# Seven half-size products summed in two pairs of PSUM banks

## The chip, the cores and the metric

The kernel runs on one core of one Trainium2 chip. The metric is the device time of one execution in microseconds. A core has five engines, each of which works off its own instructions in order: TensorE (PE, with its weight loads shown as PEld), VectorE (DVE), ScalarE (ACT), GpSimd (POOL) and SyncE (SP), whose queue issues most of the DMAs. Matmuls write only to PSUM, which here is used as eight banks of 128 x 512 float32; DVE and ACT read results from there.

## The reference

One inference step of a two-layer decoder trunk on 1056 token columns: 1024 prompt tokens and 8 sequences of 4 new tokens.

```python
def _hgrn_layer(x, g_norm, w_in, lb, o_gain, w_out, S0):
    xn = _rmsnorm(x, g_norm)
    u = (xn @ w_in).astype(jnp.float32)
    q, f, iv, gate = jnp.split(u, 4, axis=-1)
    q = jax.nn.silu(q).reshape(Bsz, T, H_B, DK_B)
    log_g = jnp.logaddexp(jnp.log(lbh), jnp.log1p(-lbh) + jax.nn.log_sigmoid(f...))
    k = -jnp.expm1(log_g)
    v = iv.reshape(Bsz, T, H_B, DV_B)
    o, S_T = _hgrn2_chunked(q, k, v, log_g, S0)
    o = o * lax.rsqrt(jnp.mean(o * o, axis=-1, keepdims=True) + EPS) * o_gain
    y = (o.reshape(Bsz, T, INNER_B) * jax.nn.silu(gate)).astype(x.dtype)
    return x + y @ w_out, S_T
```

Layer 1 is an RG-LRU layer (input projection, causal convolution, gates, scan, output projection). Layer 2 is the HGRN2 layer above: model width 1024, 8 heads, 128 keys and 128 values per head. Then comes a final RMSNorm. The change touches layer 2's input projection `xn @ w_in` and PSUM's use around it.

## The kernel before, in words

Each float32 operand is split into a high and a low part of a type that TensorE multiplies at full rate, so one product of two 128 x 128 x n blocks is three matmuls (`mm3`: high x high, high x low, low x high).

Layer 2 needs, for each head h and each of four kinds (0 query, 1 forget gate, 2 value V, 3 output gate), a product of a 1024 x 128 weight block with 1024 x 1056 activations. For most heads two kinds at a time, `a` and `b`, are done in one call of `seven`: together they form a 2 x 2 block product (two kinds, two halves of the inner dimension, two halves of 528 columns, `HT`), and it is done with seven half-size products in place of eight (Winograd's form). There are 13 calls: one for head 1 (kinds 3 and 2), two for each of heads 2 to 7. The columns of a product are again done in two parts of 264 (`QT`), x = 0 and 1; each takes twelve matmuls into one PSUM bank.

Within a call, products are numbered 1 to 7 and run in the order of a string: `GV0` (once, head 1), `FQ` (query and forget gate) and `GV` (gate and V). A "b" in the string is a place for a burst: the attention work of this head and the one before, in four bursts a head. Bursts 1 and 2 stand in the gate/V call and work on levels of this head's decay (`levels01`, `levels24`) and on the states of the head before (`states`, `advance`); bursts 3 and 4 stand in the query/forget call of the next head. In burst 2 the state matmuls come after the first half of the product that follows the "b". Masked copies (`keep`, `keep_s`, L1142 and L1145) take the level products out of PSUM.

PSUM before: the seven products rotate through three banks (`mm`), the bursts through the other five (`hg`). Each half of a product is read as soon as it is done: product 1 by an ACT copy (L1570), the others by a DVE addition `plus` (L1598) of the bank and an earlier partial sum in SBUF, written back to SBUF. The partial sums lie in six places of 264 columns in one large tile `KR` (shown as k). Product 5 has two additions per half, the others one, so a call has 14 additions and 2 copies. The last additions for V write V itself (`VT`). `ending` and `settle` then apply the activation on ACT from the finished sum in SBUF: Silu for query and gate (L1612), a Tanh and two scalings for the forget gate (L1606 to L1608). For the query and forget kinds that waits until one or two bursts have passed, since the bursts still read the rows to be overwritten. `own_gate` (L1150, DVE) multiplies the finished query by the decay.

Weights come by four DMAs per call into five raw places (`rawq`); DVE forms the sums that the seven products need (`combine`), ACT casts each to its high part (L1522), POOL subtracts to get the low part (L358). `NW` = 4 of these pairs are ahead; the next split is put in line after each product.

The order on each engine is written out by a planner, class `Flow`. Every operation is added with its engine, an assumed duration, and the keys that it reads and writes. PE's operations run in program order; the others are ordered by list scheduling with due times found backwards from the end, and additions and activations of the seven products have the first priority (0). The plan is made anew when the operations change. An operation's real waits come from the tiles that it touches. Layer 1 uses the four `mm` banks as a ring of four; after the seven products the output projection uses a ring of three (`banks8[:NMM]`).

Of the kernel before, what the change touches and what calls it, by code (L numbers as in the profile page):

```python
# [27 lines left out]
K1 = 5  # L28
NMM = 3
HC = 2  # L30
NM7 = 3
GV0, FQ, GV = "126b743b5", "12b675b43", "126b754b3"
CUT = 2
SPOTS, SPOTS0, SPOTS1 = (-1, -1, 0, 2), (2, 5, -1, -1), (1, 5, 9, 13, 17, 20)
K2 = 8 - K1
# [5 lines left out]
SEQ = 1024  # L41
# [8 lines left out]
H = 8  # L50
# [187 lines left out]
def tile_trunk(ctx: ExitStack, tc: tile.TileContext, xT, prm, hc, w0, wg, wo0, w1, wo1, s_in,  # L238
# [25 lines left out]
    def chunk(c):  # L264
        return slice(c * CH, (c + 1) * CH)

    def mm3(out, w, xh, xl, first, last):
        wh, wl = w
        T.matmul(out, wh, xh, start=first, stop=False)  # L269
        T.matmul(out, wh, xl, start=False, stop=False)  # L270
        T.matmul(out, wl, xh, start=False, stop=last)  # L271

    def run(*gens):
        for g in gens:
            for _ in g:
                pass
# [53 lines left out]
    with ExitStack() as l0:  # L330
# [9 lines left out]
        def banks(tag, n):  # L340
            return cycle([(psum.tile([128, 512], F32, tag=tag, bufs=n, name=tag), (tag, i)) for i in range(n)])
# [4 lines left out]
        def act(n, emit, r, w, prio=5, more=0.0):  # L346
            fl.add("ACT", 0.08 + 0.00086 * n + more, emit, r, w, prio)
# [47 lines left out]
        sgr = cycle(slots)  # L395
        YH = [fixed(f"yh{j}", [128, TOK], F32R) for j in range(3)]
        YL = [fixed(f"yl{j}", [128, TOK], F32R) for j in range(3)]
        mm, hg = banks("mm", 4), banks("hg", 4)

        def xpart(j, i, c):  # L400

# [603 lines left out]
    with ExitStack() as l1:  # L1005
# [488 lines left out]

        def seven(h, a, b, order, at=()):

            nonlocal rawq, places
            bursts, passed, postponed, rest = iter(at), 0, [], None

            def ending(i, *args):  # L1500
# [38 lines left out]
            combine("12", "12", "11", ALU.subtract)  # L1539
            for p in steps[2:NW]:  # L1540
                split(p)
            late, mid, low = places
            places = low, mid, late
            for c in order:
                if not c.isdigit():
                    rest = next(bursts)()
                    passed += 1
                    flush()
                    continue
                p = int(c)  # L1550
                if p == steps[-1]:
                    rawq = freed
                hi, lo, wk = parts[p]
                for x in range(2):
                    ps, pk = next(mm)
                    ops = [operand(p, j, x) for j in range(4)]

                    def emit(ps=ps, ops=ops, hi=hi, lo=lo):
# [8 lines left out]
                    z = ps[:, :QT], pk  # L1567
                    first, second = x * QT, HT + x * QT
                    if p == 1:
                        act(QT, lambda o=late[x][0], z=z[0]: S.copy(o, z), (pk,), (late[x][1],), 0)  # L1570
                    elif p == 2:
                        plus(mid[x], z, late[x])
                        ending(a, first, *mid[x])
                    elif p == 6:
                        plus(late[x], z, late[x])
                    elif p == 7:
                        plus(low[x], z, late[x])
                    elif p == 3:
                        plus(late[x], z, late[x])
                    else:  # L1580
                        t, o = second if p == 5 else first, mid[x] if next(q for q in steps if q in (4, 5)) == p else low[x]
                        if b == 2:
                            plus((VT[:, t:t + QT], ("VT", t // QT)), z, low[x])
                            if t + QT == TOK:
                                thrice("vs", VT[:, SEQ:], (("VT", 3),))
                        else:
                            plus(o, z, low[x])
                            ending(b, t, *o)
                        if p == 5:
                            plus(late[x], z, late[x])  # L1590
                    if p == [q for q in steps if q in (3, 5)][1]:
                        ending(a, second, *late[x])
                n = steps.index(p) + NW
                if n < 7:
                    split(steps[n])

        def plus(o, z, u):
            dve(QT, lambda: V.tensor_tensor(o[0], z[0], u[0], op=ALU.add), (z[1], u[1]), (o[1],), 0)  # L1598

        def settle(h, i, a, c, ck):  # L1600

            q = slice(a, a + QT)
            if i == 1:
                b, bk = brow(h, 1)
                b, bk, g = b[:, q], bk[a // QT::4], ("G", a // QT)
                act(QT, lambda: S.activation(b, c, AF.Tanh, scale=0.5), (ck,), bk, 0)  # L1606
                act(QT, lambda: S.activation(Gs[:, q], b, AF.Identity, bias=lbc[:, h:h + 1], scale=lc[:, h:h + 1]), bk, (g,), 0, 0.2)
                act(QT, lambda: S.activation(b, b, AF.Identity, bias=lc[:, h:h + 1], scale=lcn[:, h:h + 1]), bk, bk, 0, 0.2)  # L1608
            else:
                o, k = (SG[h], ykeys(h % 2, a, QT)) if i else arow(h, 0)  # L1610
                k = k if i else k[a // QT::4]
                act(QT, lambda: S.activation(o[:, q], c, AF.Silu), (ck,), k, 0)  # L1612


        dma(si.rearrange("p b v -> p (b v)"), s_in[0], (), two("si"), 4, 512)
# [34 lines left out]
        places = []  # L1650
        for i in range(6):
            key = ("s", i)
            inherit(key, [("k", j) for j in range(5) if j * CH < (i + 1) * QT and (j + 1) * CH > i * QT])
            places.append((KR[:, i * QT:i * QT + QT], key))
        places = places[:2], places[2:4], places[4:]
        rawq = [next(raws) for _ in range(NRAW)]
        for i in range(5 - NRAW):
            key = ("W", i)
# [42 lines left out]
        own = []  # L1701
        for i, o in enumerate(ks):
            key = ("k", i, 1)
            inherit(key, [("s", j) for j in range(6) if j * QT < (i + 1) * CH and (j + 1) * QT > i * CH])
# [239 lines left out]
```

## Time and profile before

| | us |
|---|---|
| median of three runs | 1028.95 |
| lowest, highest | 1027.11, 1031.18 |
| span of the profiled execution | 1027.8 |
| TensorE busy in it | 1015.8 |
| VectorE busy | 808.0 |
| ScalarE busy | 573.2 |
| GpSimd busy | 504.2 |

For the profiled execution the span is given, from its first to its last instruction; no other time of it is listed. The calls of `seven` lie at about 559 to 906 us. In the rows of the profile, "line engine op out<-in shapes xcount | busy us, mean ns of one | idle time of the engine before them <- what ended it" is a group; a timeline row is "start us, duration us, engine line op"; a row of stretches is "from:to length, then busy us (x instructions) of PE, PEld, DVE, ACT, POOL, then TensorE's granted clock, DMA share and GB/s". An engine line with q (SPq) is its queue. The names before and after "<-" are tiles; mm and hg are PSUM.

### The profile page before, as it was taken

To read this page: it belongs to the slowest core of one execution; us is meant where nothing else is said; L and a number is where in the kernel's file an instruction comes from. 1 tells how busy PE (TensorE), PEld (TensorE's weight loads), DVE (VectorE), ACT (ScalarE), POOL (GpSimd) and SP (SyncE) were. 2 spreads that over 40 slices of the span, in tenths; PEclk is the share of its full clock that TensorE was granted. 3 is DMA by queue.
4 is the path that set the end of the run, shared out by engine and by line. 5 is a ranking of instruction groups with operands and counts; after the bars stand their busy time and mean duration, and the time that the engine had idled before them with its cause. 6 is when DMAs were issued, how large, how long until landed. Compare 5 with 4: busy or idle time off the path is not lost.

```text
span 1027.8 us, 26439 instructions
## 1 busy us (share of the span) xinstructions
PE 1015.8 (99%) x10100; PEld 995.2 (97%) x10100; DVE 808.0 (79%) x1640; ACT 573.2 (56%) x1313; POOL 504.2 (49%) x580
## 2 busy tenths in 40 slices
PE   9999999999999999999999999999999999999997
PEld 9999999999999999999999999999999999999986
DVE  7998987689788689344598989888989898986436
ACT  7688566877765766344454463626363545552324
POOL 1324454454446345635425555555565656633544
PEclk9999999999999999999999999999999999999999
DMA  9211112213762487553564245443535353777204
GB/s 303 73 51 37 54 57 66 79 53 104 222 198 70 131 267 241 157 173 130 159 192 136 72 131 149 130 148 112 167 107 172 94 166 114 217 230 229 88 1 169
DMA packets 109582, 139.95 MB, mean 136 GB/s; under 512 B 24208, under 2 KB 86800, under 8 KB 109456
## 3 DMA queue, kind: packets, MB, share of 16 engines
q1 hardware_dynamic: 107440, 135.84, 42.7%
q10 hardware_dynamic: 2016, 2.43, 0.7%
q8 instruction: 79, 1.29, 0.5%
q14 instruction: 47, 0.39, 0.1%
HBM read 90.02 MB, written 41.61 MB: 128 GB/s over the span
## 4 chain that ended last, share of the span: by engine, by line
PE 87%; DVE 4%; DMA 4%; ACT 2%; issue 1%; POOL 1%; SPq 1%; POOLq 0%; ACTq 0%; DVEq 0%
PE mm L269 25%; PE mm L271 24%; PE mm L270 24%; PE hg L1138 2%; DMA R<-td 1%; PE hg L269 1%; PE hg L270 1%; PE hg L271 1%; PE hg L1340 1%; PE hg L1285 1%; PE hg L1342 1%; DMA wraw<-in_w_dram 1%; DMA k<-x1a 1%; SPq L344 1%; DMA R<-in_xT_dram 1%
## 5 line engine op out<-in xcount | busy, mean ns | idle before, releaser
L269 PE MATMUL mm<-xh,whi 128*128 128x352 f32 (+1 forms) x1127 | 349.9, 311 | 0.0
L271 PE MATMUL mm<-xh,wlo 128*128 128x352 f32 (+1 forms) x1127 | 347.8, 309 | 0.0
L270 PE MATMUL mm<-xl,whi 128*128 128x352 f32 (+1 forms) x1127 | 347.7, 309 | 0.0
L358 POOL TENSOR_TENSOR wlo<-wraw,whi 128x256 fp32r<-128x256 f32 (+3 forms) x188 | 201.9, 1090 | 194.6 <-ACT whi L418 93.7
L269 PEld LDWEIGHTS mm<-xh,whi 128*128 128x128 f32 x1127 | 211.7, 188 | 1.2 <-DVE k L1598 0.2
L270 PEld LDWEIGHTS mm<-xl,whi 128*128 128x128 f32 x1127 | 212.3, 188 | 0.4
L271 PEld LDWEIGHTS mm<-xh,wlo 128*128 128x128 f32 x1127 | 212.0, 188 | 0.0
L269 PE MATMUL mm<-t,whi 128*128 128x264 f32 (+1 forms) x330 | 96.6, 293 | 0.0
L544 DVE SCALAR_TENSOR_TENSOR k<-xb,prm_sb,k 128x352 f32<-128x352 f32 (+2 forms) x144 | 87.3, 633 | 10.4 <-ACT k L541 9.6
L271 PE MATMUL mm<-t,wlo 128*128 128x264 f32 (+1 forms) x330 | 94.5, 286 | 0.0
L270 PE MATMUL mm<-t,whi 128*128 128x264 f32 (+1 forms) x330 | 94.3, 286 | 0.0
L1598 DVE TENSOR_TENSOR k<-mm,k 128x264 f32<-128x264 f32 x154 | 64.1, 424 | 11.9 <-PE mm L271 10.5
L358 POOL TENSOR_TENSOR wlo<-R,whi 128x256 fp32r<-128x256 f32 x70 | 57.1, 838 | 27.8 <-ACT whi L1522 24.6
L1522 ACT CAST whi<-wraw 128x512 fp32r<-128x512 f32 x56 | 34.6, 617 | 58.6 <-DVE wraw L1532 31.0
L637 POOL TENSOR_TENSOR k<-X 128x352 f32<-128x352 f32 x36 | 43.8, 1222 | 45.4 <-DVE R L638 33.6
L269 PEld LDWEIGHTS mm<-t,whi 128*128 128x128 f32 x330 | 62.0, 188 | 2.1 <-ACT kt L1355 0.9
L271 PEld LDWEIGHTS mm<-t,wlo 128*128 128x128 f32 x330 | 62.2, 188 | 0.0
L270 PEld LDWEIGHTS mm<-t,whi 128*128 128x128 f32 x330 | 62.1, 188 | 0.0
L418 ACT CAST whi<-wraw 128x512 fp32r<-128x512 f32 (+2 forms) x79 | 43.8, 571 | 27.3 <-PE mm L270 20.0
L269 PE MATMUL mm<-yh,whi 128*128 128x352 f32 x153 | 49.9, 326 | 1.0 <-DVE k L689 1.0
L270 PE MATMUL mm<-yl,whi 128*128 128x352 f32 x153 | 49.4, 323 | 0.0
L271 PE MATMUL mm<-yh,wlo 128*128 128x352 f32 x153 | 49.4, 323 | 0.0
(484 smaller groups left out, 2503.1 us busy)
## 6 DMA issues: line engine op xcount, KB each, us to landing
wraw<-in_w_dram SPq DMA_DIRECT2D x89, 256.0 KB, 3.1
wraw<-in_wo_dram SPq DMA_DIRECT2D x34, 192.0 KB, 2.6
R<-in_w_dram SPq DMA_DIRECT2D x17, 256.0 KB, 3.5
si<-in_s_in_dram SPq DMA_DIRECT2D x8, 512.0 KB, 5.5
vt<-sg SPq DMA_DIRECT2D x8, 512.0 KB, 3.7
kt<-kt SPq DMA_DIRECT2D x8, 512.0 KB, 3.3
sg<-vt SPq DMA_DIRECT2D x32, 128.0 KB, 2.9
kt<-kt SPq DMA_DIRECT2D x32, 128.0 KB, 4.5
```

The source lines that it names most:

```text
L269: T.matmul(out, wh, xh, start=first, stop=False)
L270: T.matmul(out, wh, xl, start=False, stop=False)
L271: T.matmul(out, wl, xh, start=False, stop=last)
L344: fl.add("SP" if q is Q else "ACT", us, lambda: q.dma_start(dst, src), r, w, prio, kb * (1.0 if r else 0.75))
L358: emit = lambda: e.tensor_tensor(b, x, a.bitcast(F32), op=ALU.subtract)
L418: act(m, lambda hi=hi, raw=raw, m=m: S.copy(hi[:, :m], raw[:, :m]), rk, (hk,), prio)
L544: dve(u, lambda src=src, dst=dst, sh=sh, k=k: V.scalar_tensor_tensor(dst, sh(src, k), pc("cw", 12 * k + m), dst, op0=ALU.mult, op1=ALU.add ...
L637: pool(CH, lambda x=x, a=a, b=b: G.tensor_tensor(x, a.bitcast(F32), b.bitcast(F32), op=ALU.add), (ak, bk), (xk,), 3)
L1138: T.matmul(ps[32 * j:32 * j + 32, n * w:n * w + w], B[:, o:o + 32], q(slice(o, o + 32)), start=True, stop=True, tile_position=(0, 32 * j))
L1285: T.matmul(ps[w, n * 128:(n + 1) * 128], kt[:, 4 * i + n, a], vt[:, 4 * i + n], start=True, stop=True, tile_position=(0, 32 * a))
L1522: act(512, lambda: S.copy(hi, raw), (rk,), (hk,), 2)
L1598: dve(QT, lambda: V.tensor_tensor(o[0], z[0], u[0], op=ALU.add), (z[1], u[1]), (o[1],), 0)
```

## The change

The seven products of a call are summed in two pairs of PSUM banks. Products 1, 6, 7 and 4 go to one pair ("chain"), 2, 5 and 3 to the other ("side"). Only 1, 2 and 5 start afresh; the others add onto what lies in the pair. Bank 0 of a pair holds x = 0, bank 1 x = 1, and one instruction reads both (528 columns). ACT copies the pair out after 1, after 6 and after the first of 5 and 7; DVE adds the pair to an SBUF sum after 2, after 3 and after the second of 5 and 7: three additions a call. After 4 the sum is complete in PSUM and its activation reads it from there. Chain and side change places from call to call. The partial sums have three places of 528 columns. All of `settle` works on 528 columns, and V is written by an ACT copy.

Around it: the seven products have four banks (`NM7`) and the bursts four; `burst2` takes its third bank after the level products; the orders of the products are others; in each call the two kinds have changed places (forget gate and V are now `a`, which is finished by products 2 and 3; query and gate are `b`, finished by 5 or 7, and 4). The four `mm` banks are allocated as two tiles of two banks.

```diff
-NM7 = 3
-GV0, FQ, GV = "126b743b5", "12b675b43", "126b754b3"
+NM7 = 4
+GV0, FQ, GV = "126b754b3", "12b657b34", "126b573b4"
...
-        mm, hg = banks("mm", 4), banks("hg", 4)
+        PP = [psum.tile([128, 2, 512], F32, tag="mm", bufs=2, name="mm") for _ in range(2)]
+        mm, hg = cycle([(PP[i // 2][:, i % 2], ("mm", i)) for i in range(4)]), banks("hg", 4)
...
         def burst2(h):
             s = next(hg)
+            run(together([levels24(h, *s)] if h < H else []))
             t = next(hg) if h < H else s
-            run(together([levels24(h, *s)] if h < H else []))
...
-            late, mid, low = places
-            places = low, mid, late
+            one, two_, five = places
+            banks2 = [(PP[i], [("mm", 2 * i), ("mm", 2 * i + 1)]) for i in range(2)]
+            chain_, side = banks2[turns % 2], banks2[1 - turns % 2]
+            turns += 1
...
+            def copied(o, z):
+                act(HT, lambda: S.copy(halved(o[0]), z[0][:, :, :QT]), z[1], (o[1],), 0)
+            def plus(o, z):
+                dve(HT, lambda: V.tensor_tensor(halved(o[0]), z[0][:, :, :QT], halved(o[0]), op=ALU.add), (*z[1], o[1]), (o[1],), 0)
...
+                z = chain_ if p in (1, 6, 7, 4) else side
                 for x in range(2):
-                    ps, pk = next(mm)
+                    ps, pk = z[0][:, x], z[1][x]
...
-                            mm3(ps[:, :QT], (hi[:, w], lo[:, w]), uh, ul, j == 0, j == 3)
+                            mm3(ps[:, :QT], (hi[:, w], lo[:, w]), uh, ul, j == 0 and p in (1, 2, 5), j == 3, p not in (1, 2, 5))
...
+                if p == 1:
+                    copied(one, z)
+                elif p == 2:
+                    plus(one, z)
+                    ending(a, 0, halved(one[0]), [one[1]])
+                elif p == 6:
+                    copied(two_, z)
+                elif p in (5, 7):
+                    if five in ready:
+                        plus(five, z)
+                        ending(b, HT, halved(five[0]), [five[1]])
                     else:
+                        copied(five, z)
+                        ready.append(five)
+                elif p == 3:
+                    plus(two_, z)
+                    ending(a, HT, halved(two_[0]), [two_[1]])
+                else:
+                    ending(b, 0, z[0][:, :, :QT], z[1])
...
+            elif i == 2:
+                act(HT, lambda: S.copy(halved(VT[:, q]), c), ck, [("VT", x), ("VT", x + 1)], 0)
+                if a:
+                    thrice("vs", VT[:, SEQ:], (("VT", 3),))
...
-                seven(h, 0, 1, FQ, (lambda h=h: burst3(h - 1), lambda h=h: burst4(h - 1)))
+                seven(h, 1, 0, FQ, (lambda h=h: burst3(h - 1), lambda h=h: burst4(h - 1)))
                 own_gate(h)
-            seven(h, 3, 2, GV if h >= HC else GV0, (lambda h=h: burst1(h), lambda h=h: burst2(h)))
+            seven(h, 2, 3, GV if h >= HC else GV0, (lambda h=h: burst1(h), lambda h=h: burst2(h)))
```

More of the change, by code (lines that the diff above doesn't have):

```diff
@@ L265, in chunk, with mm3 @@
         return slice(c * CH, (c + 1) * CH)
-    def mm3(out, w, xh, xl, first, last):
+    def mm3(out, w, xh, xl, first, last, skip=False):
         wh, wl = w
-        T.matmul(out, wh, xh, start=first, stop=False)
-        T.matmul(out, wh, xl, start=False, stop=False)
-        T.matmul(out, wl, xh, start=False, stop=last)
+        T.matmul(out, wh, xh, start=first, stop=False, skip_group_check=skip)
+        T.matmul(out, wh, xl, start=False, stop=False, skip_group_check=skip)
+        T.matmul(out, wl, xh, start=False, stop=last, skip_group_check=skip)
     def run(*gens):
@@ L1495, in seven @@
         def seven(h, a, b, order, at=()):
-            nonlocal rawq, places
+            nonlocal rawq, turns
             bursts, passed, postponed, rest = iter(at), 0, [], None
@@ L1566, in seven @@
                         rest = None
[L1567 to L1579, printed above, removed]
-                    else:
[L1581 to L1592, printed above, removed]
+                if p == 1:
[9 more added lines that the diff above has]
+                        ending(b, HT, halved(five[0]), [five[1]])
+                    else:
+                        copied(five, z)
[5 more added lines that the diff above has]
+                    ending(b, 0, z[0][:, :, :QT], z[1])
                 n = steps.index(p) + NW
@@ L1595, in seven, with halved @@
                     split(steps[n])
-        def plus(o, z, u):
-            dve(QT, lambda: V.tensor_tensor(o[0], z[0], u[0], op=ALU.add), (z[1], u[1]), (o[1],), 0)
+        def halved(o):
+            return o.rearrange("p (x n) -> p x n", x=2)
         def settle(h, i, a, c, ck):
-            q = slice(a, a + QT)
+            q, x = slice(a, a + HT), a // QT
+            own = lambda k: [*k[x::4], *k[x + 1::4]]
             if i == 1:
                 b, bk = brow(h, 1)
[L1605 to L1608, printed above, removed]
-            else:
-                o, k = (SG[h], ykeys(h % 2, a, QT)) if i else arow(h, 0)
-                k = k if i else k[a // QT::4]
-                act(QT, lambda: S.activation(o[:, q], c, AF.Silu), (ck,), k, 0)
+                b, bk, g = halved(b[:, q]), own(bk), [("G", x), ("G", x + 1)]
+                act(HT, lambda: S.activation(b, c, AF.Tanh, scale=0.5), ck, bk, 0)
+                act(HT, lambda: S.activation(halved(Gs[:, q]), b, AF.Identity, bias=lbc[:, h:h + 1], scale=lc[:, h:h + 1]), bk, g, 0, 0.2)
+                act(HT, lambda: S.activation(b, b, AF.Identity, bias=lc[:, h:h + 1], scale=lcn[:, h:h + 1]), bk, bk, 0, 0.2)
+            elif i == 2:
+                act(HT, lambda: S.copy(halved(VT[:, q]), c), ck, [("VT", x), ("VT", x + 1)], 0)
+                if a:
+                    thrice("vs", VT[:, SEQ:], (("VT", 3),))
+            else:
+                o, k = (SG[h], ykeys(h % 2, a, HT)) if i else arow(h, 0)
+                act(HT, lambda: S.activation(halved(o[:, q]), c, AF.Silu), ck, k if i else own(k), 0)
         dma(si.rearrange("p b v -> p (b v)"), s_in[0], (), two("si"), 4, 512)
@@ L1649, in tile_trunk @@
         mm, hg = cycle(banks8[:NM7]), cycle(banks8[NM7:])
-        places = []
-        for i in range(6):
+        places, turns = [], 0
+        for i in range(3):
             key = ("s", i)
-            inherit(key, [("k", j) for j in range(5) if j * CH < (i + 1) * QT and (j + 1) * CH > i * QT])
-            places.append((KR[:, i * QT:i * QT + QT], key))
-        places = places[:2], places[2:4], places[4:]
+            inherit(key, [("k", j) for j in range(5) if j * CH < (i + 1) * HT and (j + 1) * CH > i * HT])
+            places.append((KR[:, i * HT:i * HT + HT], key))
         rawq = [next(raws) for _ in range(NRAW)]
@@ L1703, in tile_trunk @@
             key = ("k", i, 1)
-            inherit(key, [("s", j) for j in range(6) if j * QT < (i + 1) * CH and (j + 1) * QT > i * CH])
+            inherit(key, [("s", j) for j in range(3) if j * HT < (i + 1) * CH and (j + 1) * HT > i * CH])
             own.append((o[0], key))
```

3 lines of the change are left out of this document (2 added, 1 removed).

## The prediction

> **What bounds the kernel now.** I read the page first, then the busy time by stretches, then TensorE's own waits, then the timeline around one wait. Here is the head of the page, with its slices and its chain.
>
> ```profile
> span 1027.8 us, 26439 instructions
> PE 1015.8 (99%) x10100; PEld 995.2 (97%) x10100; DVE 808.0 (79%) x1640; ACT 573.2 (56%) x1313; POOL 504.2 (49%) x580
> PE   9999999999999999999999999999999999999997
> DVE  7998987689788689344598989888989898986436
> PE 87%; DVE 4%; DMA 4%; ACT 2%; issue 1%; POOL 1%; SPq 1%; POOLq 0%; ACTq 0%; DVEq 0%
> ```
>
> TensorE (PE) is busy for 99% of the span and owns 87% of the chain that ended last. VectorE (DVE) shows 9 and 8 in the slices of the seven-product stage, from about 560 to 905 us, so it is nearly full there as well. The next view says which of the two sets the pace. Its columns are PE, PEld, DVE, ACT and POOL.
>
> ```profile
> 620.00:680.00 60.00, 60.00 (x934) 58.44 (x933) 52.58 (x114) 27.84 (x74) 35.19 (x43) 1.00 0.50 149
> 740.00:800.00 60.00, 60.00 (x998) 58.27 (x987) 55.73 (x122) 29.71 (x79) 34.77 (x43) 1.00 0.43 130
> 1000.00:1027.80 27.80, 20.73 (x158) 19.39 (x156) 16.84 (x38) 12.75 (x32) 13.72 (x18) 0.92 0.45 156
> ```
>
> In the stage that changes, PE is busy 60.00 of 60.00 us at clock 1.00. DVE's 52.58 to 55.73 lies beside it. Only the last 27.8 us have real room, 7.1 us. A busy PE need not be at its peak, so I looked for waits hidden inside it. PE's waits from 560 to 910 us are one row, and the timeline (PE and DVE) shows what the one disturbed seam between product halves looks like.
>
> ```profile
> PE hg L1190 <- issue: 0.7, 1, 0.7
> ...
> 655.25 0.29 PE L271 MATMUL mm<-t,wlo 128*128 128x264 f32 x1
> 655.37 0.29 PE L269 MATMUL mm<-t,whi 128*128 128x264 f32 x1
> 655.57 0.43 DVE L1598 TENSOR_TENSOR k<-mm,k 128x264 f32<-128x264 f32 x1 [0.18 <-PE mm L271]
> ...
> 678.29 0.29 PE L271 MATMUL mm<-t,wlo 128*128 128x264 f32 x1
> 678.71 0.48 DVE L1403 SCALAR_TENSOR_TENSOR sg<-a,prm_sb,sg 128x256 f32<-128x256 f32 x1 [1.81 <-DMA a<-on]
> 681.03 0.43 DVE L1598 TENSOR_TENSOR k<-mm,k 128x264 f32<-128x264 f32 x1
> 681.22 0.28 PE L271 MATMUL mm<-xh,wlo 128*128 128x264 f32 x1
> 681.51 0.39 PE L269 MATMUL mm<-xh,whi 128*128 128x264 f32 x1
> ```
>
> Undisturbed matmuls start 0.12 us apart (655.25 to 655.37) although each lasts 0.28, also across the seam between two halves. So a half of twelve takes 1.47 us and a product 2.93. At the seam at 655 an addition starts 0.03 us after the last matmul of its half ends (655.54, 655.57). At 681.51 PE starts 0.05 us after an addition ends (681.46), 0.29 after the matmul before instead of 0.12: that addition came late, and cost PE 0.17. In 345 us this stage loses under 1 us to waits. DVE is full but not what PE waits for.
>
> **The change part by part.** Each duration is from the one profiled execution. No time of that execution beside its span of 1027.8 is shown; the span lies 1.15 us under the median of the three runs, 1028.95, and I add the terms to the median.
>
> ```profile
> L1598 DVE TENSOR_TENSOR k<-mm,k 128x264 f32<-128x264 f32 x154 | 64.1, 424 | 11.9 <-PE mm L271 10.5
> L1598 DVE TENSOR_TENSOR sg<-mm,k 128x264 f32<-128x264 f32 x28 | 11.9, 424 | 0.2
> L753 DVE TENSOR_TENSOR sg<-mm,sg 128x352 f32<-128x352 f32 x21 | 11.0, 523 | 30.6 <-PE mm L271 30.5
> L1570 ACT COPY k<-mm 128x264 f32<-128x264 f32 x26 | 9.7, 376 | 7.9 <-PE mm L271 7.8
> L1088 ACT COPY sg<-mm 128x352 f32<-128x352 f32 x3 | 1.3, 449 | 0.0
> L1612 ACT ACTIVATE sg<-k 128x264 f32<-128x264 f32 x28 | 10.7, 417 | 7.1 <-DVE k L1598 6.6 <-DMA yd<-sg 0.5
> L1608 ACT ACTIVATE a<-a,smalls 128x264 f32<-128x264 f32 x24 | 14.0, 600 | 0.3
> ```
>
> *VectorE.* 154 + 28 = 182 additions, 14 in each of 13 calls, go: 182 x 0.424 = 77.2 us. In come 3 x 13 = 39 of 528 columns. From 264 to 352 columns the rows grow by 0.099 us, so 264 more give 0.424 + 3 x 0.099 = 0.72 us, an estimate that counts the second bank as plain columns: 28.1 us. DVE is relieved of 49 us, and all of that lay beside a full PE: 0 on the path.
>
> *ScalarE.* By the two copy rows 264 more columns cost 0.22 us (0.073 x 3), so a copy of 528 takes 0.60. 26 copies of 264 go (9.8), 39 of 528 come (23.4), and 14 for V, which DVE used to write (8.4). The Tanh (about Silu's 0.42) and two scalings (0.60) of the forget gate become half as many and 0.22 longer: 24 x 1.62 = 38.9 becomes 12 x 2.28 = 27.4. 52 Silus of 0.42 (21.8) become 26 of 0.64 (16.6). Net +5 us on an engine busy 28 of 60: 0 on the path.
>
> *TensorE.* The same matmuls in another order; those of products 3, 4, 6 and 7 add onto what is there. The trace has no accumulation across products, but in every product eleven of twelve matmuls already add, at the same 0.12 us. I price it at 0.
>
> *The waits it adds.* A product now needs its whole pair of banks read, and one instruction reads both, so nothing is read before the second half is done. Where one product lies between two on the same pair, the read may use 2.93 - 0.16 (the last matmul's tail) - 0.03 - 0.05 = 2.69 us. It takes 0.72 on DVE or 0.60 on ACT, which leaves 1.97 or 2.09 for the queue ahead of it. In the steady orders "12b657b34" and "126b573b4" the pairs always alternate, and one pass ends on the pair that the next does not begin with. I price these at 0; if that cover goes, see the third rival. Two seams have no product between:
>
> (a) "126b754b3", used once, ends on 3, on the side pair, which becomes the next call's chain pair: 0.16 + 0.03 + 0.72 + 0.05 = 0.96 us, plus whatever DVE is in.
>
> (b) The very last product 4 is on the pair whose first bank the output projection's ring takes first (148 turns of that ring in layer 1 are a multiple of four). There the gate's Silu reads the sum: 0.16 + 0.03 + 0.64 + 0.05 = 0.88, plus whatever ACT is in.
>
> "In" is bounded by nothing at all and by the longest instruction, 1.57 us (DVE, next fence) or 0.82 (a scaling of 528). I take 0.3 at each, half of a common one (0.70, 0.61), as both instructions have first priority. Sum 2.4. The "7" right behind "6" in "126b754b3" is covered by a burst of 1.1 us (622.44, next fence) and adds a few tenths at most.
>
> ```profile
> 622.44 1.10 PE L1138 MATMUL mm<-R,a 128*32 128x64 f32 x64
> 640.52 0.61 ACT L1522 CAST whi<-wraw 128x512 fp32r<-128x512 f32 x1
> 641.21 1.91 POOL L358 TENSOR_TENSOR wlo<-wraw,whi 128x256 fp32r<-128x256 f32 x2 [0.84 <-ACT whi L1522]
> 649.13 1.25 DVE L1241 STREAM_TRANSPOSE sg<-sg 128x1024 f32<-128x1024 f32 x1 [0.22 <-PE hg L1340]
> 668.84 1.57 DVE L1150 TENSOR_TENSOR R<-R,ST 128x1056 f32<-128x1056 f32 x1 [0.52 <-ACT R L1612]
> 680.41 0.70 DVE L1120 TENSOR_TENSOR a<-a,ST 128x528 f32<-128x528 f32 x1
> ```
>
> *Moved work.* V is now ready after products 2 and 3 instead of 5 and 4. Its small transpose and four DMAs on SP's queue move with it, to where SP already carries four weight loads per call. Their reader is the next head's first burst, eleven products (32 us) later. The head before must have given V up by then: its transpose (1.25) stands in burst 4, four products (11.7 us) ahead. Splits of weights change order, not number: a cast of 0.61 and two POOL subtractions of 1.9 together, three products (8.8 us) ahead of use. The query half that ends last needs a Silu and then the own gate, 1.57, before burst 1, three products later: 2.2 against 8.8.
>
> *One bank less for the bursts.* Their ring falls from five to four, and burst 2 takes its banks in another order. Its states and sample product now reuse banks that burst 2's own level products filled.
>
> ```profile
> 633.16 0.88 PE L1138 MATMUL hg<-R,sg 128*32 128x32 f32 x59
> 635.97 0.20 DVE L1145 COPY_PREDICATED attns<-mask,hg 32x32 f32<-32x32 uint8 x1
> 636.49 0.46 DVE L1142 COPY_PREDICATED attnd<-mask,hg 128x256 f32<-128x256 uint8 x1
> 638.47 0.44 DVE L1142 COPY_PREDICATED attnd<-mask,hg 128x256 f32<-128x256 uint8 x1
> 638.16 0.50 PE L1315 MATMUL hg<-vb,kst 96*128 96x512 f32 x1
> ```
>
> Today the masked copies out of the level bank end at 638.91, 4.9 us after its matmuls (634.04), while the sample product starts at 638.16. In the new ring it takes that very bank. So the copies must come 0.8 us sooner. The order is planned anew with that need known, and DVE has 49 us less, about 3.8 per call, so I take 0 and keep 0.8 per head as the other end.
>
> *Gains.* At most the 0.17 at 681 and the 0.7 of issue: I take 0.1. **Sum:** 1028.95 + 2.4 - 0.1 = 1031.2.
>
> [...] At (a) a half-size addition, as today, would free the first bank during the second half, and by the rows above there would be no wait; as one instruction it costs the 0.96. [...]
>
> **The rivals.**
>
> *Bursts run short of banks (slower).* If the new order keeps the copies where they are, PE stands 638.91 + 0.05 - 638.16 = 0.8 us in burst 2 of each of seven heads, 5.6 us in all: 1036.8. It decides once the copies end over 4.1 us after the level products. For it: today's order. Against it: DVE is relieved and the planner sees the bank. [...]
>
> *Merging makes it faster.* It needs 5.1 us, and PE's waits hold under 1 in the stage. Only the tail's 7.1 us could give more, if a relieved DVE brought the last outputs sooner; but no seven-product addition is in that stretch. At its point, 1023.8.
>
> *An addition is late in DVE's queue.* The addition ready at 678.58 began at 681.03, 2.45 late, behind an instruction that waited 1.81 for a DMA. With only 1.97 of room that would cost 0.48; at product 3 of "12b657b34", in six heads, 2.9: 1034.1, on the edge of slower. Against it: fewer instructions queue.
>
> *The pair counts as one buffer.* Were waits kept per pair and not per bank, each second product of layer 1 would wait for its predecessor's evacuation, 74 x (0.16 + 0.03 + 0.52 + 0.05) = 56 us: 1085. Against it: today the additions write pieces of one tile (k) while others read its neighbours, with no wait for it in PE's rows.
>
> **How the numbers follow.** 0.5%, 5.1 us, is about what a measurement of this kernel can tell from no change. Forecast (0 to +5) 0.70; short banks 0.14; late additions 0.08; faster 0.05; pair as one 0.03. Slower is 0.14 + 0.03 and a third of 0.08, 0.20; faster 0.05; same 0.75. The low end, 1026.5, has neither new wait (-2.4), loses today's 0.9 of waits and takes 1.5 for the scatter of the runs (1027.11 to 1031.18). The high end, 1037.5, is short banks and 0.7 of the same scatter. Some 0.15 is left out.
>
> **What would show it.** Right: additions x39 at about 0.72 us, DVE near 759 and ACT near 578 us, PE's busy time within 1 us of 1015.8, 60.00 of 60.00 in mid-stage, and two new PE waits of 0.9 to 1.6 us, one on an addition, one on a Silu. Short banks would show as PE or its weight loads waiting on L1142 or L1145 in every head. The forecast is wrong if PE's waits repeat per head, or if the 0.12 between matmuls changes.

## The result and the profile after

The changed kernel takes 1099.07 us (median of 4 runs, 1097.10 to 1100.76) against 1029.59 for the kernel before on the same chip (4 runs, 1027.11 to 1031.18): a ratio of 1.067 [1.065, 1.069]. The prediction of 1031.2 with a range to 1037.5 was wrong by 68 us. The profiled execution has a span of 1095.1 and a time of 1097.1.

The head of the page after, with the slices of PE and the chain that ended last:

```profile
PE 1039.2 (95%) x10100; PEld 1006.2 (92%) x10100; DVE 772.5 (71%) x1497; ACT 582.4 (53%) x1278; POOL 496.1 (45%) x580
PE   9999998999998899899999899999999999999996
PE 79%; DVE 10%; ACT 5%; DMA 3%; issue 2%; POOL 1%; SPq 0%; POOLq 0%; ACTq 0%; DVEq 0%
```

PE's share of the chain fell from 87% to 79%, DVE's rose from 4% to 10%. The eights in PE's line stand in the first 23 of the 40 slices of 27.4 us, and the seven-product stage, which the change is about, begins in the 23rd, at 609. The view by stretches says the same in numbers (columns PE, PEld, DVE, ACT, POOL, granted clock, DMA share, GB/s):

```profile
60.00:420.00 360.00, 339.64 (x2014) 333.27 (x2013) 262.27 (x471) 231.81 (x457) 147.02 (x165) 0.97 0.33 98
420.00:480.00 60.00, 54.23 (x321) 52.78 (x321) 34.74 (x57) 26.40 (x57) 32.75 (x36) 0.97 0.53 172
740.00:800.00 60.00, 60.00 (x1043) 58.22 (x1045) 47.69 (x92) 31.49 (x71) 32.99 (x41) 1.00 0.42 130
```

In layer 1, which the change touches only by how its four banks are allocated, PE is idle for 20 of 360 us and for 6 of 60. Before, the same two stretches read:

```profile
60.00:420.00 360.00, 358.01 (x2217) 356.24 (x2216) 293.26 (x518) 251.85 (x498) 170.69 (x188) 1.00 0.39 119
420.00:480.00 60.00, 60.00 (x375) 59.58 (x374) 26.57 (x54) 23.17 (x51) 30.19 (x30) 1.00 0.52 173
```

In mid-stage PE is as full as before (60.00 of 60.00 at 740), and DVE's share there has fallen from 55.73 to 47.69. To place the 67 us I cut every execution at the starts of the first and the last matmul of 264 columns, which exist in the seven-product stage alone:

| us | up to the stage | the stage | from its end | span |
|---|---|---|---|---|
| before | 559.4 | 346.6 | 121.8 | 1027.8 |
| after | 609.4 | 352.7 | 132.9 | 1095.1 |
| difference | +50.1 | +6.1 | +11.1 | +67.3 |

PE's waits name what ends the idle time in layer 1: not operands, but readers of the product banks (DVE's addition at L754, ACT's copy and activation at L529 and L575).

```profile
PE mm L269 <- DVE sg L754: 9.5, 11, 3.3
PE mm L269 <- ACT xb L529: 6.9, 3, 3.0
PE mm L269 <- ACT sg L575: 5.8, 4, 4.1
```

The timeline around one of them:

```profile
465.39 0.33 PE L271 MATMUL mm<-yh,xl 128*128 128x352 f32 x1
465.75 0.52 DVE L754 TENSOR_TENSOR sg<-mm,sg 128x352 f32<-128x352 f32 x1 [2.85 <-PE mm L271]
466.33 0.43 PE L269 MATMUL mm<-yh,xh 128*128 128x352 f32 x1 [0.62 <-DVE sg L754]
```

A product ends at 465.72, its addition runs from 465.75 to 466.27, and only then does the next product start, although it writes the other bank of the pair, whose own last use, by the order of the ring, lies four products back. Matmuls of 352 columns otherwise start 0.16 us apart (on plain float32, as at 442.68 in the kernel before, one takes 0.59 by the starts around it); here 0.94 pass, so 0.78 is lost. The same wait stands at 459.65 and 473.03, at every second product. That is the fourth rival of the prediction, with its price of 0.16 + 0.03 + 0.52 + 0.05 = 0.76 almost to the digit.

Not every loss in layer 1 is 0.78. Up to the stage some 30 waits of more than 0.5 us make 37 us, and 7 of them, each over 1.5, make half of that. In the longest, on PE and ACT, the reader stood in its engine's queue behind other work:

```profile
173.16 0.32 PE L271 MATMUL hg<-X,gl 128*128 128x352 f32 x1
...
175.75 1.28 ACT L575 ACT_TABLE_LOAD   x1
177.04 0.46 ACT L575 ACTIVATE sg<-mm 128x352 f32<-128x352 f32 x1
...
177.56 0.66 PE L269 MATMUL mm<-xh,whi 128*128 128x352 f32 x1 [4.07 <-ACT sg L575]
178.02 0.49 PE L270 MATMUL mm<-xl,whi 128*128 128x352 f32 x1
178.31 0.49 PE L271 MATMUL mm<-xh,wlo 128*128 128x352 f32 x1
```

ACT loaded a table ahead of the activation, PE stood for 4.07, and behind it the matmuls start 0.29 us apart where 0.16 is usual. The granted clock (the third number from the end) shows why:

```profile
178.00:184.00 6.00, 6.00 (x23) 6.00 (x23) 0.00 (x0) 2.70 (x7) 1.32 (x2) 0.53 0.32 95
```

From 184 us on it is 1.00 again. Behind five more of the 7 long waits stands a stretch of half clock, each 3.4 or 6.8 us long. In these six stretches some 90 matmuls start late, by 0.13 us each: 12 us more. Taken against the usual spacing, all the starts up to the stage come 57 us late in sum, against 9 in the kernel before: that is nearly all of the 50 that layer 1 lost. The wait of 4.07 was followed by a clock of 0.53, and waits of 1.91, 1.92 and 1.97 us were followed by half clock (0.50) too; the last section has more on it.

The stage's 6.1 us are three waits. Here are PE's waits from 609 to 963 us:

```profile
PE mm L269 <- ACT k L1550: 2.8, 1, 2.8
PE mm L269 <- DVE k L1553: 2.6, 1, 2.6
PE mm L270 <- DVE xl L358: 1.0, 1, 1.0
```

The first, at 622.34, is product 7 right behind product 6, on the same pair; PE starts 2.91 us late there. The second, at 642.88, is seam (a) of the prediction (2.76 late), and the third, at 628.79, is an operand that came late (1.12). The stage before had lost 1.0.

### The profile page after: what moved, and what is told of

It reads as the page before. It is cut to its first block, busy times and chain, and to the rows that moved or that the text cites. A ratio compares the mean times of both kernels' runs of the same rounds, so it can differ in the third digit from the quotient of the medians.

```text
span 1095.1 us, 26141 instructions
## 1 busy us (share of the span) xinstructions
PE 1039.2 (95%) x10100; PEld 1006.2 (92%) x10100; DVE 772.5 (71%) x1497; ACT 582.4 (53%) x1278; POOL 496.1 (45%) x580
## 4 chain that ended last, share of the span: by engine, by line
PE 79%; DVE 10%; ACT 5%; DMA 3%; issue 2%; POOL 1%; SPq 0%; POOLq 0%; ACTq 0%; DVEq 0%
PE mm L269 23%; PE mm L271 22%; PE mm L270 22%; PE hg L1139 2%; DVE k L545 1%; PE hg L1341 1%; PE hg L1286 1%; PE hg L1343 1%; PE hg L269 1%; PE hg L271 1%; PE hg L270 1%; DMA R<-td 1%; DVE sg L1130 1%; DVE R L659 1%; ACT k L542 1%
## 5 line engine op out<-in xcount | busy, mean ns | idle before, releaser
L269 PE MATMUL mm<-xh,whi 128*128 128x352 f32 (+1 forms) x1127 | 356.6, 316 | 20.8 <-ACT xb L529 6.9
L270 PE MATMUL mm<-xl,whi 128*128 128x352 f32 (+1 forms) x1127 | 352.4, 313 | 1.0 <-DVE xl L358 1.0
L271 PE MATMUL mm<-xh,wlo 128*128 128x352 f32 (+1 forms) x1127 | 352.0, 312 | 0.0
L358 POOL TENSOR_TENSOR wlo<-wraw,whi 128x256 fp32r<-128x256 f32 (+2 forms) x204 | 208.5, 1039 | 221.9 <-ACT whi L419 110.7
L269 PEld LDWEIGHTS mm<-xh,whi 128*128 128x128 f32 x1127 | 215.3, 191 | 26.8 <-ACT xb L529 7.7
L270 PEld LDWEIGHTS mm<-xl,whi 128*128 128x128 f32 x1127 | 215.9, 192 | 1.4 <-DVE xl L358 1.2
L271 PEld LDWEIGHTS mm<-xh,wlo 128*128 128x128 f32 x1127 | 215.7, 191 | 0.0
L1523 ACT CAST whi<-wraw 128x512 fp32r<-128x512 f32 x64 | 39.6, 621 | 55.0 <-PE mm L270 21.9
L358 POOL TENSOR_TENSOR wlo<-R,whi 128x256 fp32r<-128x256 f32 x54 | 48.5, 918 | 29.5 <-ACT whi L1523 29.5
L1553 DVE TENSOR_TENSOR k<-mm,k 128x528 f32<-128x528 f32 x39 | 27.5, 705 | 35.4 <-PE mm L271 35.2
```

The source lines that it names most:

```text
L269: T.matmul(out, wh, xh, start=first, stop=False, skip_group_check=skip)
L270: T.matmul(out, wh, xl, start=False, stop=False, skip_group_check=skip)
L271: T.matmul(out, wl, xh, start=False, stop=last, skip_group_check=skip)
L358: emit = lambda: e.tensor_tensor(b, x, a.bitcast(F32), op=ALU.subtract)
L1523: act(512, lambda: S.copy(hi, raw), (rk,), (hk,), 2)
L1553: dve(HT, lambda: V.tensor_tensor(halved(o[0]), z[0][:, :, :QT], halved(o[0]), op=ALU.add), (*z[1], o[1]), (o[1],), 0)
```

## The experiments

Each was timed beside the kernel before. The table gives times and the three parts as above; the texts follow.

| | time | ratio to before, 95% | to the stage | stage | output | span |
|---|---|---|---|---|---|---|
| after | 1099.07 | 1.067 [1.065, 1.069] | 609.4 | 352.7 | 132.9 | 1095.1 |
| e1 allocation only | 1124.25 | 1.093 [1.091, 1.095] | 608.0 | 378.8 | 136.9 | 1123.7 |
| e2 interleaved ring | 1061.46 | 1.032 [1.030, 1.034] | 584.1 | 349.5 | 124.9 | 1058.5 |
| e3 four one-bank tiles | 1035.47 | 1.006 [1.005, 1.008] | 559.1 | 346.3 | 129.0 | 1034.4 |
| e4 e2, other seams | 1061.58 | 1.032 [1.031, 1.034] | 586.5 | 351.4 | 124.9 | 1062.8 |
| e5 pairs in layer 2 only | 1035.43 | 1.006 [1.004, 1.007] | 558.6 | 349.9 | 124.0 | 1032.5 |
| e6 bank split only | 1029.74 | 1.000 [0.999, 1.001] | 558.2 | 346.2 | 123.9 | 1028.3 |
| e7 e3, last order | 1030.07 | 1.000 [0.999, 1.001] | 559.6 | 346.3 | 122.5 | 1028.4 |
| e8 e5, roles not changed once | 1033.43 | 1.004 [1.003, 1.006] | 559.2 | 345.7 | 126.8 | 1031.6 |
| e9 e8, places moved | 1035.10 | 1.006 [1.004, 1.007] | 559.2 | 347.0 | 127.8 | 1034.1 |
| e10 e8, last order | 1029.41 | 1.000 [0.999, 1.001] | 559.3 | 346.2 | 122.2 | 1027.7 |

**e1: the kernel before with the allocation alone.**

```diff
-        mm, hg = banks("mm", 4), banks("hg", 4)
+        PP = [psum.tile([128, 2, 512], F32, tag="mm", bufs=2, name="mm") for _ in range(2)]
+        mm, hg = cycle([(PP[i // 2][:, i % 2], ("mm", i)) for i in range(4)]), banks("hg", 4)
```

> The kernel before with one edit: the four banks of the ring mm are allocated as two tiles of two banks. No sums, orders or reads change. Theory 1 (a pair counts as one buffer: a product into one bank of a pair waits until the other bank of the pair has been read): layer 1 loses 48 to 50 us as in the changed kernel, where its products reach the seven-product stage at 609.4 instead of 559.4 us. In the stage itself the ring of three has two banks of one pair, so one half in three waits 0.16 + 0.03 + 0.42 + 0.05 = 0.66 us plus VectorE's queue, some 0.5: 61 x 1.2 = 70 us; the output projection about 12. In all about 1160 us (1120 to 1200). Rival (the loss comes from layer 2's new sums, orders and reads): 1029 us within 5.

1124.25 us. The same operations on the same four banks in the same rotation, and layer 1 loses 48.6 us as it does after. What differs is that two banks are one tile. The seven-product stage, whose additions still read bank by bank, loses 32 us, less than half of what was expected of it. PE's waits there come to 24 us, and about half of them are on those additions:

```profile
PE mm L269 <- DVE k L1599: 12.7, 15, 1.9
```

Most of the others are on readers of the bursts' results: in this kernel the stage's products have three of the four banks, and the fourth, which shares a tile with the third, serves the bursts. So in this program the wait goes by the tile.

**e2: the changed kernel, consecutive products on different pairs outside the seven.**

```diff
-NMM = 3
+NMM = 4
-        mm, hg = cycle([(PP[i // 2][:, i % 2], ("mm", i)) for i in range(4)]), banks("hg", 4)
+        mm, hg = cycle([(PP[i // 2][:, i % 2], ("mm", i)) for i in (0, 2, 1, 3)]), banks("hg", 4)
```

> The changed kernel with the ring mm in another order: bank 0 of pair 0, bank 0 of pair 1, bank 1 of pair 0, bank 1 of pair 1, and four banks in it (not three) outside the seven products. So a product shares its pair with the one before the last, not with the last. Theory 1: the pair's read has a whole product (2.4 us or more) to end in, the waits are covered; the seven-product stage begins at 559 us within 2 and the output stage takes 122 us within 2 again; the stage itself keeps its 6 us: 1035 us (1031 to 1040). Rival: still above 1090 us.

1061.46, not 1035. Half of the loss in layer 1 stays. A product now waits for the reader of the product before the last, and that reader is not always done after one product. The largest row of its waits before the stage:

```profile
PE mm L269 <- DVE k L690: 5.7, 3, 3.1
```

A ring of four separate banks gives a reader the time of three products. The interleaved pairs give it one, and that is too little here.

**e3: the changed kernel with four tiles of one bank, each bank read by an instruction of its own.** Sums in PSUM, orders of products, four banks for the bursts and three places stay; a call then has six additions and six copies of 264 columns.

```diff
-        PP = [psum.tile([128, 2, 512], F32, tag="mm", bufs=2, name="mm") for _ in range(2)]
+        BB = [(psum.tile([128, 512], F32, tag="mm", bufs=4, name="mm"), ("mm", i)) for i in range(4)]
+        mm, hg = cycle(BB), banks("hg", 4)
...
-                dve(HT, lambda: V.tensor_tensor(halved(o[0]), z[0][:, :, :QT], halved(o[0]), op=ALU.add), ...
+                for x, (ps, pk) in enumerate(z):
+                    u = o[0][:, x * QT:x * QT + QT]
+                    dve(QT, lambda u=u, ps=ps: V.tensor_tensor(u, ps[:, :QT], u, op=ALU.add), (pk, o[1]), (o[1],), 0)
```

> The changed kernel with four tiles of one bank; the sums stay in PSUM, in the same order, but each bank is read by an instruction of its own (264 columns): six additions and six copies per call, and two Silus for product 4. Theory 1: no shared waits anywhere, layer 1 and the output stage as before; the waits at the two seams nearly go, since the first half's bank is read while the second half runs: 1030 us (1026 to 1034), the stage 347 us within 2. Rival (sums in PSUM, the orders or four banks for the bursts cost the time): above 1085 us.

1035.47, above the range expected. Layer 1 and the stage are what they were before (559.1 and 346.3), and both seams are gone. The 7.2 us are behind the stage, at the start of the output projection:

```profile
905.35 0.28 PE L271 MATMUL mm<-t,wlo 128*128 128x264 f32 x1
908.09 0.42 PE L269 MATMUL mm<-xh,t 128*128 128x352 f32 x1 [2.45 <-ACT xh L1710]
910.35 0.66 PE L270 MATMUL mm<-xl,t 128*128 128x352 f32 x1 [1.84 <-DVE xl L358]
```

Two waits make 4.3 us, and behind them the granted clock is 0.50 from 908.80 to 915.60 (0.94 in the mean of 860 to 920). The projection's first operands are loaded into `KR`, where the partial sums lay. In the last call 7 runs ahead of 3, so the third place is free only after 7 and its activation, a Silu that ends at 902.87. Two loads go out at 903.30, the first fence (e3, ACT and SP's queue); in the kernel before, the second fence, three went out together from 900.37.

```profile
902.23 0.64 ACT L1628 ACTIVATE sg<-k 128x528 f32<-128x528 f32 x1
903.30 0.86 SPq L344 DMA_DIRECT2D k<-yd  x2
```

```profile
900.37 2.03 SPq L344 DMA_DIRECT2D k<-yd  x3
```

**e4: e2 with other seams.**

```diff
-GV0, FQ, GV = "126b754b3", "12b657b34", "126b573b4"
+GV0, FQ, GV = "126b573b4", "12b657b34", "126b573b4"
...
-        mm, hg = cycle(banks8[:NMM]), cycle(banks8[NMM:])
+        mm, hg = cycle(banks8[1:NMM] + banks8[:1]), cycle(banks8[NMM:])
```

> As e2_interleaved, and two edits at the seams: the string of head 1 is also 126b573b4, so that it ends on 4 and the next call begins on the other pair, and the output ring begins with a bank of the pair that the last product 4 doesn't use. If the stage's loss is the wait at these seams (2.8 and 0.9 us in the changed kernel's trace), this is 3 to 4 us faster than e2_interleaved: 1031 us (1028 to 1035), with no wait of PE on an addition over 0.5 us. If that wait only moves to another product: the same as e2_interleaved.

1061.58, as e2. Of the waits on sums one of 0.83 is left in the stage, where product 5 of the first call follows product 2 on the same pair (e2 had 2.91 and 0.70), and operands of product 5 (2.21) and of the output projection (1.07) came late in their place. The edit moved two things at once (the order of the first call and the ring behind the last), so it says only that a seam can be exchanged for another wait; e8 takes the first seam away without touching an order.

**e5: pairs in layer 2 alone.**

```diff
-NMM = 3
+NMM = 4
...
+        pm = l0.enter_context(tc.tile_pool(name="pm", bufs=1, space=PSUM))
+        mm = cycle([(pm.tile([128, 512], F32, tag="mm", bufs=4, name="mm"), ("mm", i)) for i in range(4)])
...
+        pp = l1.enter_context(tc.tile_pool(name="pp", bufs=1, space=PSUM))
+        PP = [pp.tile([128, 2, 512], F32, tag="pp", bufs=2, name="pp") for _ in range(2)]
+        banks8 = [(PP[i // 2][:, i % 2], ("mm", i)) for i in (0, 2, 1, 3)] + [next(hg) for _ in range(4)]
```

> Layer 1's four product banks are four tiles of their own again, in a pool that is released before layer 2; the two pairs exist in layer 2 alone, used there as in the change, with the order (0,0),(1,0),(0,1),(1,1) of e2 outside the seven-product stage. If the wait for the pair's other bank is the whole of what layer 1 lost, the stage begins where it begins in the kernel before (559.4, at most 561 with the heads of layer 2 on interleaved pairs), the stage takes e2's 349.5 and the output its 124.9: a span of 1034, a time of about 1035 (1032 to 1039), ratio 1.006. If layer 1 lost its 50 us to something else that the change does there, the start stays past 580 and the time past 1055.

1035.43, as expected in all three parts. With the two-bank tiles out of layer 1 its 50 us are back. What is left is the two seams of the prediction. The first, on PE and DVE (the line numbers of this kernel are 3 higher than after's):

```profile
584.73 0.28 PE L271 MATMUL pp<-xh,wlo 128*128 128x264 f32 x1
...
584.97 1.00 DVE L1124 TENSOR_TENSOR a<-sg 128x512 f32<-128x512 f32 x1
585.89 0.33 DVE L1310 SCALAR_TENSOR_TENSOR a<-a,gp,hg 128x128 f32<-128x128 f32 x1
...
587.18 0.70 DVE L1556 TENSOR_TENSOR k<-pp,k 128x528 f32<-128x528 f32 x1
...
587.93 0.39 PE L269 MATMUL pp<-xh,whi 128*128 128x264 f32 x1 [2.92 <-DVE k L1556]
```

The sum is complete at 585.01, and its addition begins at 587.18. An instruction of 1.00 and five small ones of burst 2 stand ahead of it on DVE. PE starts 3.08 us late, and half clock behind the wait, matmuls 0.22 apart instead of 0.12, costs some 1.5 more by estimate (last section).

**e6: the kernel before with only the bank split changed.**

```diff
-NM7 = 3
+NM7 = 4
...
             s = next(hg)
-            t = next(hg) if h < H else s
             run(together([levels24(h, *s)] if h < H else []))
+            t = next(hg) if h < H else s
```

> The kernel before with only the split of the eight banks in the stage changed: four for the products, four for the bursts (three and five before), and burst 2 taking its second bank later, as the change has it; sums, additions and orders as before. If the bursts' fourth bank cover is enough (the price of 0 in the prediction): 1028.8, within 0.3%. If the bursts miss their fifth bank (the prediction's other end, 0.8 us a head over 6 heads): about 1033.5, with the added waits at products on the bursts' banks in the stage.

1029.74, ratio 1.0004 [0.9994, 1.0014]. Four banks are enough for the bursts, and a fourth for the products brings nothing.

**e7: e3 with another order in the last call.**

```diff
-            seven(h, 2, 3, GV if h >= HC else GV0, ...
+            seven(h, 2, 3, GV0 if h < HC else GV if h < H - 1 else "126b537b4", ...
```

> e3 (four banks each a tile of its own) with the last call of the stage alone in the order 1, 2, 6, 5, 3, 7, 4, so that the second place of the sums comes free one product earlier than the third, and three whole chunks of the rows that the output projection's loads land in are free before product 7. If e3's 7.3 us in the output stage came from those late loads (two waits of 2.62 and 2.10 at its start and what followed them), the output stage comes back to about 122 and the time to 1029 (1027 to 1032), start and stage staying at 559 and 346. If they came from the merged Silu of 528 columns or from anything else in the scheme, the output stage stays near 129 and the time at 1035.

1030.07. The output stage is back at 122.5, and the three loads go out together, 6.6 us ahead of e3's 903.30:

```profile
896.68 1.92 SPq L344 DMA_DIRECT2D k<-yd  x3
```

**e8: e5, and the pairs keep their roles once, after the first call.**

```diff
-            turns += 1
+            turns += 1 + (order == GV0)
```

> e5 with one edit: after the first call, the only one whose order ends on the side pair, the pairs do not change roles, so that the second call's product 1 goes to the pair that product 4 used and not to the one that product 3's addition has yet to read. The same turn of roles puts the very last product 4 on the pair that the output projection's ring takes second. No order of products changes. If the two seams are what e5 has left over the kernel before, the wait of 3.08 at the first seam shrinks to 0.1 to 0.3 (its read ended 3.0 after product 3, and product 1 now covers 2.93), that of 0.87 at the output goes, the stage takes 347 and the time is about 1031 (1029.5 to 1033). If the waits only move to what is late next, as in e4, where operands of product 5 and of the output projection came late, the time stays at 1034 to 1036 with waits on casts in place of those on the sums.

The first seam is gone as expected, and the stage takes 345.7. Yet the time is 1033.43, just above the range expected. The wait on the last sum at the output is gone too, but the output projection's first operands are late in its place, and behind these waits the granted clock is 0.50 from 908.40 to 911.70 (matmuls of 352 columns start 0.29 apart). PE's waits from 558 to 1000 us are one row, on the splits of those operands:

```profile
PE pp L270 <- DVE xl L358: 2.1, 2, 1.3
```

**e9: e8 with the first-finished sum beside the unused columns of `KR`.**

```diff
-            one, two_, five = places
+            two_, five, one = places
```

> e8 with one edit: the sum that is finished first (product 2's) lies in the third of the three places in KR, beside the 176 columns of KR that no place uses, so that two whole chunks of 352 for the output projection's loads are free after product 2 in place of one; the other two sums take the first and second place. If e8's remaining 5 us against the kernel before are the output projection's late loads (its two waits of 1.31 and 0.84 on splits at the start), the output stage falls from 126.7 to 122 to 124 and the time to 1030 (1028.5 to 1031.5). If the output stage is longer for another reason (two-bank reads there, other queues), it stays near 126.5 and the time near 1033.5.

1035.10: a miss. One more load goes out early, and the projection still waits for a split, 2.04 where e8's two waits made 2.15. How many chunks are free early is not by itself what decides.

```profile
910.07 0.43 PE L270 MATMUL pp<-xl,t 128*128 128x352 f32 x1 [2.04 <-DVE xl L358]
```

**e10: e8 with e7's order of products in the last call.** It is the change in the stage, with its two-bank sums and single additions, and of the waits that it brought only two of 0.2 us are left from 558 to 1000 us.

```diff
-            seven(h, 2, 3, GV if h >= HC else GV0, ...
+            seven(h, 2, 3, GV0 if h < HC else GV if h < H - 1 else "1265b37b4", ...
```

> e8 with the last call of the stage alone in the order 1, 2, 6, 5, 3, 7, 4, as in e7, with the second-to-last burst between 5 and 3, which lie on the same pair. The two places whose chunks the first loads take are then free before product 7. If what e7 mended in the single-bank version is also what e8 has left, the output stage falls from 126.7 to about 122 and the time to 1029.5 (1028 to 1031.5), the pairs then costing nothing at all against the kernel before. If the output's start depends on how the order of splits falls out and not on the loads' places, as e9's miss would have it, the output stays at 126 to 128 and the time at 1033 to 1035.

1029.41, ratio 1.0003 [0.9994, 1.0012]. Every part is within 0.4 us of the kernel before, and PE is busy for 1015.9 as it was for 1015.8, beside a DVE with 28 us less to do:

```profile
PE 1015.9 (99%) x10100; PEld 995.2 (97%) x10100; DVE 780.1 (76%) x1497; ACT 585.2 (57%) x1278; POOL 497.0 (48%) x580
```

No version beats the kernel before.

## Why the prediction was wrong

*The step that failed is the chance of the fourth rival.* "The pair counts as one buffer" had its place (each second product of layer 1), its price (56 us) and its time (1085; 1087 if counted from 1031.2 as the other rivals are), and a chance of 0.03. It was set aside with "today the additions write pieces of one tile (k) while others read its neighbours". Those rows are about a tile in SBUF that DVE and ACT use; PE's matmuls in the rows shown read other tiles, so its rows could not show such a wait. And in the kernel before every PSUM tile is one bank, so nothing there could show how a tile of two is treated. The question was unobserved and cost 56 us if it went wrong: its bound belonged in the range. e1 and e5 show it from both sides: the allocation alone costs layer 1 48.6 us of its 50, and taking it out of layer 1 gives them back.

*The price of that rival was right in kind and short in total.* 0.78 a wait against 0.76. Layer 1 lost 50.1 against 56, but not as 74 equal waits: 19 were of 0.7 to 0.9, 7 were 1.6 to 4.2 long, and the half clock behind six of those added 12. The output stage, also on a ring through pairs, lost 11 more, which the rival left out.

*Seam (a): the term was mis-sized.* 0.96 + 0.3 was forecast; 2.76 was lost after, 3.08 in e5. The addition took 0.69, near its 0.72, but began 1.8 us late after (642.13, its sum complete at 640.28), not 0.3. Ahead of it DVE worked off one instruction of 0.90 and six of 0.34, from 639.76 on; I counted half an instruction there, not the run of burst work that the plan had placed. The bound of one instruction of 1.57 was also read too low: in the stage before, one at 586.91 (L1120) takes 2.61. The wait after:

```profile
640.00 0.28 PE L271 MATMUL mm<-xh,wlo 128*128 128x264 f32 x1
...
642.13 0.69 DVE L1553 TENSOR_TENSOR k<-mm,k 128x528 f32<-128x528 f32 x1
...
642.88 0.39 PE L269 MATMUL mm<-xh,whi 128*128 128x264 f32 x1 [2.60 <-DVE k L1553]
```

*The 7 right behind 6 was mis-sized.* "A few tenths at most" was forecast behind the burst; 2.91 was lost after, more than at seam (a). The sum of product 6 was complete at 618.40, and its copy began at 621.69. On ACT, ahead of the copy, stood two casts that waited 5.03 for DVE, which was held by one instruction of 6.63:

```profile
613.55 6.63 DVE L1130 TENSOR_TENSOR sg<-ST 128x528 f32<-128x528 f32 x1
...
621.03 0.76 ACT L1471 CAST xh<-sg 128x264 fp32r<-128x264 f32 x2 [5.03 <-DVE sg L1468]
621.69 0.59 ACT L1550 COPY k<-mm 128x528 f32<-128x528 f32 x1
...
622.34 0.39 PE L269 MATMUL mm<-t,whi 128*128 128x264 f32 x1 [2.79 <-ACT k L1550]
```

In e5 the same string runs, that instruction takes 1.25, and PE loses nothing there, so the forecast holds where DVE is not held up. Why the instruction took 6.63 is not shown.

*Seam (b) was right*: 0.86 lost against 0.88, on the Silu that reads the pair. The queue term of 0.3 did not occur.

```profile
962.16 0.28 PE L271 MATMUL mm<-t,wlo 128*128 128x264 f32 x1
962.48 0.61 ACT L1621 ACTIVATE sg<-mm 128x528 f32<-128x528 f32 x1 [0.86 <-PE mm L271]
...
963.14 0.43 PE L269 MATMUL mm<-xh,t 128*128 128x352 f32 x1 [0.70 <-ACT sg L1621]
```

*The terms at 0 were right.* DVE's relief brought nothing: e10 has it and is at 1.0003. Accumulation across products cost nothing: mid-stage PE 60.00 of 60.00, and e10's stage takes 346.2. Four banks for the bursts cost nothing (e6), so the first rival is dead. The third, an addition late in DVE's queue, did not come at product 3 of every head: PE's only wait on an addition in the stage is at seam (a), where this mechanism enlarged the term. The sizes of the merged instructions were close:

```profile
L1553 DVE TENSOR_TENSOR k<-mm,k 128x528 f32<-128x528 f32 x39 | 27.5, 705 | 35.4 <-PE mm L271 35.2
L1550 ACT COPY k<-mm 128x528 f32<-128x528 f32 x39 | 23.4, 599 | 37.3 <-PE mm L271 37.3
```

0.705 against 0.72, 0.599 against 0.60; ACT 582.4 against 578. DVE came to 772.5 against 759: the additions took what was forecast, so its other instructions took 13 us more in all, off the path in mid-stage. The 6.63 above, where 1.25 is usual, is 5.4 of them; the rest is not explained.

*What the prediction did not name:* the output projection's first loads take the places of the partial sums. With fewer, larger places and 7 ahead of 3 in the last call they came late; the waits on them and the half clock behind cost 7 us in e3 and 5 in e8. In e7 and e10 the order of the last call alone mended it. That e9's way did not leaves open which part of the order matters, the place that comes free or the burst and activations that move with it.

## What to carry to other kernels

When two buffers become one tile, ask for every user of either part, in every stage, what it will now wait for; the stages that the change is not about pay as well. Where before shows no row for such a wait, a cheap argument from another memory is no evidence, and the whole price belongs in the range. A ring's worth is the time it gives a reader until its buffer is written again: count it in products (three with four separate banks, one with two alternating pairs, none inside a pair; up to the stage the last two took 25 and 50 us more here, in e2 and after), and set it against the reader's queue and not only its duration.

## What was not expected of the hardware

A wait of 4.07 us on PE (after, up to 177.56) cost more than itself: from 178 to 184 us the granted clock was 0.53, and matmuls of 352 columns started 0.29 apart instead of 0.16. But the length of the wait alone does not decide it: in the same trace waits of 1.91, 1.92 and 1.97 in layer 1 were followed by half clock, and 2.79 and 2.60 in the stage were not. Half clock began inside the wait of 4.07, at 176.9, but in e5 it came later than the wait: PE waits 2.92, and the first matmuls behind the wait start 0.12 us apart; from 589.43 on they start 0.22 apart.

In the trace of after, half clock begins at 176.9, 258.8, 340.7, 357.8, 371.4, 453.3 and 1088.2 us, always a multiple of 3.41 us apart, and up to the stage it lasts one or two such steps. PE had been idle for more than half of the step just before each of the first six. Three steps, each followed by the one behind it: after, behind the wait of 1.91; after, behind seam (a); e5, behind seam (a).

```profile
255.37:258.78 3.41, 1.52 (x9) 1.52 (x10) 3.11 (x7) 2.52 (x8) 0.55 (x2) 1.00 0.07 18
258.78:262.19 3.41, 3.41 (x14) 3.41 (x13) 3.41 (x11) 2.64 (x4) 0.00 (x0) 0.50 0.28 78
```

```profile
641.08:644.49 3.41, 1.61 (x13) 1.61 (x14) 3.41 (x12) 0.63 (x1) 1.41 (x3) 1.00 0.21 77
644.49:647.90 3.41, 3.41 (x30) 3.41 (x30) 0.69 (x5) 1.12 (x2) 0.55 (x1) 1.00 0.33 101
```

```profile
585.85:589.26 3.41, 1.33 (x10) 1.33 (x11) 3.41 (x14) 0.63 (x1) 1.96 (x3) 1.00 0.00 0
589.26:592.67 3.41, 3.41 (x18) 3.41 (x17) 1.13 (x6) 0.08 (x1) 0.00 (x0) 0.51 0.58 176
```

In the steps before those six PE was busy for 0.05 to 1.52 us of the 3.41, in the one before the kernel before's only half clock (from 1023.3) for 1.43. Behind steps with 1.61 and 1.69 (after, from 641.08 and 620.61) the clock stayed at 1.00. But two half-clock steps of after, from 180.3 and 344.1, stand behind half-clock steps with PE busy for 2.70 and 2.61, and the last half clock, from 1088.2, behind a step with 3.12. What sets the clock is not shown.
